# Ten chunks of the down projection's second column pass, beside the up projection

## The chip, the core and the metric

The kernel runs on one core of a Trainium2 chip. The metric is the device time of one launch in microseconds, as the median of several runs. The core's engines are TensorE (PE in the profile, with PEld for its weight loads), VectorE (DVE), ScalarE (ACT), GpSimd (POOL) and SyncE (SP). Each runs its own list of instructions in order and waits for others by semaphores; DMA transfers are issued here from the queues of SP and POOL.

## What is computed

One decoder layer for 256 tokens with 2048 features, in float32: a combined projection, two kinds of attention, an output projection, a LayerNorm, and a gated feed-forward network with a short causal convolution, followed by a second LayerNorm. The change lies in the feed-forward part:

```python
def conv_ffn(h, w_up, conv_w, conv_b, w_down):
    u = h @ w_up                                   # 256 x 2048 by 2048 x 11264
    g, val = u[..., :FFN_DIM], u[..., FFN_DIM:]    # FFN_DIM = 5632
    S = h.shape[1]
    gp = jnp.pad(g, ((0, 0), (CONV_W - 1, 0), (0, 0)))
    gc = conv_b + sum(conv_w[j] * gp[:, j:j + S] for j in range(CONV_W))
    return (jax.nn.silu(gc) * val) @ w_down        # 256 x 5632 by 5632 x 2048
...
h = layer_norm(DEEPNORM_ALPHA * h + mix, ln1_g[l], ln1_b[l])
f = conv_ffn(h, w_up[l], conv_w[l], conv_b[l], w_down[l])
h = layer_norm(DEEPNORM_ALPHA * h + f, ln2_g[l], ln2_b[l])
```

## The kernel before

**Precision.** Every float32 operand is split into a high part (`hi`, a rounded copy that ScalarE makes) and a low part (`lo`, the remainder, a subtraction on VectorE). A product is then three matmuls: high by high, high by low, low by high. `split_hi` and `split_lo` do this for the weights.

**The order of the work** is written out by hand. A list `stream` names the weight tiles one after another: value, query and key, output, up (88 tiles, gate and value of 44 feature blocks in turn) and down projection. A step works on one tile `i`, while the tile `i + 2` is split and `i + 5` or `i + 6` is loaded, so weights are ready two steps ahead.

**The up projection** takes 88 steps (`up_step`), each with 16 pairs of matmuls (512 and 256 columns) in `up_products`. ScalarE copies the result out of its PSUM bank (`up_copy`, tile `ub`), VectorE adds its two halves (`up_sum`), and the convolution and the gate follow (`gate_in`, `gate_taps`, `gate_out`, `act_out`). Two blocks of 128 features make a pair `p` of activations, one for every four steps, kept in a ring of three.

**The down projection** multiplies 22 pairs (chunks of 256 rows of `w_d`) by the weights, in two passes: first columns 0 to 1023 (n = 0), then 1024 to 2047 (n = 1). For one chunk and pass the product is a 2 x 2 by 2 x 2 block product. It is done either with eight block products (24 matmuls of 512 columns, `mm_d`), or, by Strassen's scheme in Winograd's form, with seven (21 matmuls), which needs four sums of weight blocks (tiles `tf`, split into `tslot`) and four sums of activations (tile `sf`, split into `sp`); `SEVEN` says which chunks do so. Seven of PSUM's banks collect the results: CB[0][0], CB[0][1], CB[1][0] and the four in MB, whose contents are shared by several outputs and added into `z` at the end of a pass by `shared_out`.

**Where the two meet.** The chunks 0 to 19 of the first pass run beside the up projection. Chunk `p` takes the four steps from 4 p + 8: `down_raw` loads its weights into one of two raw tiles (`raw` or a part of `ring`) two chunks ahead, the step before prepares the first sums, and after a step's up products TensorE runs 5, 5, 5 and 6 of the 21 side products (`down_products`, cut by `CUTS`). The three raw weight blocks that are used directly go to `rslot`, whose low parts are made by a DMA that accumulates (POOL, line 1166). `act_spill` writes the split activations (`dparts`) and, for five chunks, their split sums (`dsums`) to DRAM. After the up projection come chunks 20 and 21 of the first pass, and then the whole second pass: 22 chunks, of which five use seven products, with the activations read back by `act_back` (tiles `back`, `sback`). The last four chunks are ordered by output block, so that the LayerNorm of the first 128 tokens overlaps the end.

Two lines carry most of this:

```python
SEVEN = {"v": ((), range(1, 8, 3)), "d": (range(PT - 2), range(3, 16, 3))}
...
for j, p in enumerate((*range(PT - LATE, PT), PT - LATE - 1, *range(PT - LATE - 1))):
    stream.append(("d", p, 1, j))
```

## Time and profile before

| | us |
|---|---|
| median of 3 runs (1116.1 to 1117.8) | 1116.96 |
| the profiled execution | 1116.05 |
| its span in the profile | 1114.2 |
| TensorE busy | 1104.8 |
| VectorE busy | 853.8 |
| ScalarE busy | 681.5 |
| GpSimd busy | 57.4 |
| mean granted TensorE clock | 0.998 |

The profile comes from one execution. Its time is 1116.05 us, of which the span covers 1114.2. A row of a timeline gives the start, the duration, the engine and line, the operation and "out<-in" by the tiles' names, and how often it is repeated. A group row gives the total busy time, the mean duration in nanoseconds and the idle time ahead of it. The table of windows gives for each stretch the busy time of each engine with its count of instructions, the granted clock, the DMA engines' share and the rate. The rows themselves stand in the prediction.

### The profile page before, as it was taken

How to read it: one execution, taken by the hardware profiler on the slowest of the kernel's cores; microseconds unless marked ns; L12 is line 12 of the kernel's file. 1: busy time of each engine (PE TensorE's matmuls, PEld its weight loads, DVE VectorE, ACT ScalarE, POOL GpSimd, SP SyncE). 2: the span in 40 equal slices, each digit the busy share in tenths (PEclk: the TensorE clock that was granted, in tenths of full speed). 3: DMA queues.
4: the chain of work that ended last, by engine and by line, in shares of the span. 5: the costliest groups of instructions: out<-in, count | busy, mean ns of one | idle time of the engine just before them, and what ended most of it. 6: DMA issues, size and time to landing. Idle time of an engine off the chain costs nothing.

```text
span 1114.2 us, 15765 instructions
## 1 busy us (share of the span) xinstructions
PE 1104.8 (99%) x5929; PEld 952.9 (86%) x5929; DVE 853.8 (77%) x1400; ACT 681.5 (61%) x1077; POOL 57.4 (5%) x81
## 2 busy tenths in 40 slices
PE   9999999999999999999999999999999999999997
PEld 6888888888888898888888888888888888888886
DVE  6777778887755778888888887777777777677866
ACT  6656676655443486666666666666666666644552
POOL 0000010000000000000000000000000000001103
PEclk9999999999999999999999999999999999999999
DMA  9888866445455537877877877778777777688982
GB/s 326 286 286 308 245 195 209 151 158 183 159 182 189 189 119 260 300 247 246 275 257 257 270 246 250 250 241 261 248 249 243 247 249 245 199 321 289 330 324 77
DMA packets 59868, 266.46 MB, mean 239 GB/s; under 512 B 6080, under 2 KB 7568, under 8 KB 42000
## 3 DMA queue, kind: packets, MB, share of 16 engines
q1 hardware_dynamic: 51584, 229.81, 57.4%
q0 software_dynamic: 8064, 35.39, 14.1%
q8 instruction: 46, 0.75, 0.3%
q10 hardware_dynamic: 144, 0.26, 0.1%
q14 instruction: 30, 0.25, 0.1%
HBM read 227.93 MB, written 15.20 MB: 218 GB/s over the span
## 4 chain that ended last, share of the span: by engine, by line
PE 98%; DVE 1%; DMA 0%; ACT 0%; issue 0%; SPq 0%; DVEq 0%
PE bank L277 97%; PE bank L410 0%; DMA raw<-in_w_v 0%; PE bank L995 0%; PE bank L457 0%; ACT hf L998 0%; DVE h L1010 0%; DVE st L481 0%; DVE z L478 0%; DVE z L1357 0%; DVE z L1353 0%; DVEq L1505 0%; DVE mv L487 0%; ACT hi L208 0%; DVE h L1009 0%
## 5 line engine op out<-in xcount | busy, mean ns | idle before, releaser
L277 PE MATMUL bank<-h,hi 128*128 128x512 f32 x1376 | 480.9, 391 | 0.0
L277 PE MATMUL bank<-h,lo 128*128 128x256 f32 x1376 | 388.2, 282 | 0.0
L277 PEld LDWEIGHTS bank<-h,hi 128*128 128x128 f32 x1376 | 258.4, 188 | 54.1
L277 PEld LDWEIGHTS bank<-h,lo 128*128 128x128 f32 x1376 | 260.5, 189 | 3.7
L179 DVE TENSOR_TENSOR lo<-raw,hi 128x1024 fp32r<-128x1024 f32 x147 | 177.0, 1222 | 84.0 <-ACT hi L177 83.4
L196 DVE TENSOR_TENSOR lo<-raw,hi 128x1024 fp32r<-128x1024 f32 x171 | 207.0, 1221 | 25.0 <-ACT hi L188 24.8
L177 ACT ACTIVATE hi<-raw 128x1024 fp32r<-128x1024 f32 x155 | 161.7, 1056 | 75.8 <-PE bank L277 49.8
L277 PE MATMUL bank<-x,hi 128*128 128x512 f32 x512 | 182.9, 398 | 0.0
L188 ACT ACTIVATE hi<-raw 128x1024 fp32r<-128x1024 f32 x171 | 177.3, 1050 | 0.0
L277 PE MATMUL bank<-x,lo 128*128 128x256 f32 x512 | 144.4, 282 | 0.0
L1115 ACT ACTIVATE ub<-bank 128x512 f32<-128x512 f32 x86 | 51.4, 598 | 107.5 <-PE bank L277 104.5
L277 PEld LDWEIGHTS bank<-x,hi 128*128 128x128 f32 x512 | 96.3, 188 | 20.4 <-issue 1.0
L277 PEld LDWEIGHTS bank<-x,lo 128*128 128x128 f32 x512 | 97.0, 189 | 0.2
L1124 DVE TENSOR_TENSOR ub<-ub 128x256 f32<-128x256 f32 x86 | 36.5, 424 | 56.5 <-ACT ub L1115 56.5
L748 ACT ACTIVATE tslot<-tf 128x512 fp32r<-128x512 f32 x80 | 50.3, 629 | 44.1 <-DVE tf L1205 25.1
L751 DVE TENSOR_TENSOR tslot<-tf,tslot 128x512 fp32r<-128x512 f32 x80 | 55.3, 691 | 12.4 <-ACT tslot L748 10.3
L277 PE MATMUL bank<-hi,back 128*128 128x512 f32 (+1 forms) x216 | 59.0, 382 | 0.0
L277 PE MATMUL bank<-hi,x 128*128 128x512 f32 x208 | 55.9, 391 | 0.7 <-ACT hi L208 0.7
L277 PE MATMUL bank<-tslot,sp 128*128 128x512 f32 x180 | 47.8, 392 | 0.0
L277 PEld LDWEIGHTS bank<-hi,x 128*128 128x128 f32 x208 | 38.8, 188 | 9.6 <-ACT hi L208 1.7
L277 PEld LDWEIGHTS bank<-hi,back 128*128 128x128 f32 x216 | 40.2, 188 | 7.8
L277 PE MATMUL bank<-hi,mh 128*128 128x512 f32 x128 | 41.6, 396 | 0.0
(233 smaller groups left out, 1461.4 us busy)
## 6 DMA issues: line engine op xcount, KB each, us to landing
raw<-in_w_u SPq DMA_DIRECT2D x88, 1024.0 KB, 6.2
raw<-in_w_d SPq DMA_DIRECT2D x68, 512.0 KB, 7.3
raw<-in_w_qk SPq DMA_DIRECT2D x32, 1024.0 KB, 4.9
raw<-in_w_o SPq DMA_DIRECT2D x16, 1024.0 KB, 4.7
raw<-in_w_v SPq DMA_DIRECT2D x28, 512.0 KB, 7.3
ring<-in_w_d SPq DMA_DIRECT2D x20, 512.0 KB, 7.2
dparts<-rslot SPq DMA_DIRECT2D x20, 512.0 KB, 2.8
back<-dparts POOLq DMA_DIRECT2D x19, 512.0 KB, 7.3
```

What stands on the lines that cost most here:

```text
L177: ACT.activation(hi[:, s], t[:, x:y], AF.Copy)
L179: DVE.tensor_tensor(lo[:, s], t[:, x:y], hi[:, s].bitcast(F32), ALU.subtract)
L188: ACT.activation(hi, t[:, half * 1024:half * 1024 + 1024], AF.Copy)
L196: DVE.tensor_tensor(lo, t[:, half * 1024:half * 1024 + 1024], hi.bitcast(F32), ALU.subtract)
L277: PE.matmul(out, lhsT, rhs, start=start, stop=stop)
L748: ACT.activation(side["t"][:, 0, j], f, AF.Copy)
L751: DVE.tensor_tensor(side["t"][:, 1, j], f, side["t"][:, 0, j].bitcast(F32), ALU.subtract)
L1115: ACT.activation(t.rearrange("p j t -> p (j t)"), up_bank(i), AF.Copy)
L1124: DVE.tensor_tensor(u[:, 0], u[:, 0], u[:, 1], ALU.add)
```

## The change

Three things are changed together.

- Chunks 0 to 9 of the **second** pass now run beside the up projection's steps 8 to 45, with seven products each, in the place of the first pass; chunk 9 takes two steps instead of four. They are left out of the second pass, which keeps twelve chunks, two of them with seven products.
- At steps 46 to 49 the seven banks are added into `z` (`shared_out(1, ..., True)` and three `z_add`), while chunk 0 of the **first** pass begins. From step 50 to 87 there are then two chunks in four steps, each with 9 and 12 side products: a new one (10 to 19) with its activations at hand, and one of 1 to 9 whose activations and sums are read back from DRAM into a tile `more` (`act_reload`, POOL's queue). For these the low parts of `rslot` are made by VectorE (`r_hi`) and not by the accumulating DMA. The raw tile for the chunk after the next is asked for in a chunk's last step.
- The tiles `e0` and `e1` of the attention become places in one tile `e` (`e_place`), whose space `more` and `ends` use later; the offset `STAND_AT` of some stationary operands goes. The first sums for the last LayerNorm (`z_stats`) move two steps earlier in the shorter second pass.

```diff
-SEVEN = {"v": ((), range(1, 8, 3)), "d": (range(PT - 2), range(3, 16, 3))}
-
 LATE = 2

+EARLY = 10
+
+SEVEN = {"v": ((), range(1, 8, 3)), "d": (range(PT - LATE), (3, 6))}
...
-    for j, p in enumerate((*range(PT - LATE, PT), PT - LATE - 1, *range(PT - LATE - 1))):
+    for j, p in enumerate((*range(PT - LATE, PT), PT - LATE - 1, *range(EARLY, PT - LATE - 1))):
         stream.append(("d", p, 1, j))
...
         SP.dma_start(kept["parts"][p].bitcast(F32), side["x"].bitcast(F32))
-        if p in sevens:
+        if p < EARLY or p in sevens:
             SP.dma_start(kept["sums"][p].bitcast(F32), side["sp"].bitcast(F32))
...
-    def down_raw(p):
-        if p >= PT - 2:
+    jobs = []
+    for p in range(EARLY):
+        jobs.append((1, p, 4 * p + 8, 2 if p == EARLY - 1 else 4))
+    jobs.append((0, 0, 4 * EARLY + 6, 4))
+    for p in range(EARLY, PT - LATE):
+        jobs.append((0, p, 4 * p + 10, 2))
+        if p - EARLY + 1 < EARLY:
+            jobs.append((0, p - EARLY + 1, 4 * p + 12, 2))
+    FLUSH = EARLY
+
+    def fresh(j):
+        return jobs[j][1] >= EARLY or jobs[j][0] == 1
+
+    def steps(u):
+
+        for j, (_, _, first, length) in enumerate(jobs):
+            if first <= u < first + length:
+                k = 4 // length
+                return j, range((u - first) * k, (u - first + 1) * k)
+        return -1, range(u - 4, u - 3) if 4 <= u < 8 else range(0)
+
+    def down_raw(j):
+        if j >= len(jobs):
             return
...
+    def act_reload(j):
+
+        if j >= len(jobs) or fresh(j):
+            return
+        for t, src in zip(operands(j), (kept["parts"], kept["sums"])):
+            POOL.dma_start(t, src[jobs[j][1]])
...
-            np_ = pairs - (PAIRED_END if kind == "d" and n == 1 else 0)
+            np_ = pairs - (PAIRED_END + EARLY if kind == "d" and n == 1 else 0)
...
+    for m in (*MB, (0, 0), (0, 1), (1, 0)):
+        total[("d", "early", m) if m in MB else ("d", "early", *m)] = 3 * EARLY
...
-    CUTS = (0, 5, 10, 15, 21)
-
...
+    def cuts(j, u):
+
+        _, _, first, length = jobs[j]
+        if length == 2:
+            c = (0, 9, 21)
+        elif j == FLUSH:
+            c = (0, 0, 7, 14, 21)
+        else:
+            c = (0, 5, 10, 15, 21)
+        return c[u - first], c[u - first + 1]
...
+        if j == FLUSH and 0 in now:
+            shared_out(1, 0, True)
+        if j == FLUSH and 1 in now:
+            shared_out(1, 1, True)
+        if j == FLUSH and 2 in now:
+            for t, c in ((1, 0), (0, 0), (0, 1)):
+                z_add(1, t, c, CB[t][c])
...
+        if 3 in now:
+            down_raw(j + 2)
+        if 1 in new:
+            act_spill(jobs[j][1])
+        if 0 in now:
+            act_reload(j + 1)
...
+    def r_hi(j, x, y):
+
+        w, r = raw_of(j)[:, x:y], side["r"]
+        ACT.activation(r[:, 0, x:y], w, AF.Copy)
+        if not fresh(j):
+            DVE.tensor_tensor(r[:, 1, x:y], w, r[:, 0, x:y].bitcast(F32), ALU.subtract)
...
-                        at(i + 6 + 3 * t, z_stats, t, c, (512, 256)[t])
+                        at(i + 4 + 3 * t, z_stats, t, c, (512, 256)[t])
```

The other parts of `up_step` do what they did before, with "the chunk's step 0 to 3" (`0 in now` and so on, `now` being one or two of them) in place of "the step's place in its group of four", and with the sums of activations left out for a chunk that is read back (`new`, `fresh`).

**TensorE, in the second half of the up projection.** Before, a chunk's side products stand at the ends of four steps, after that step's matmuls with `h` (two rows of which are kept here):

```order
L277 MATMUL bank_74<-h_3405,hi 128x512
L277 MATMUL bank_74<-h_3405,lo 128x256
L277 MATMUL bank_76<-tslot,sp 128x512 x3
L277 MATMUL bank_78<-tslot,sp 128x512 x2
...
L277 MATMUL bank_78<-tslot,sp 128x512
L277 MATMUL bank_77<-tslot,sp 128x512 x3
L277 MATMUL bank_73<-tslot,rslot 128x512
...
L277 MATMUL bank_73<-tslot,rslot 128x512 x2
L277 MATMUL bank_75<-rslot 128x512 x3
```

In the changed kernel, at the ends of three steps, a new chunk's last twelve, then the first nine and the last twelve of a chunk that is read back:

```order
L279 MATMUL bank_73<-tslot,rslot 128x512 x3
L279 MATMUL bank_75<-rslot 128x512 x3
L279 MATMUL bank_71<-rslot 128x512 x3
L279 MATMUL bank_72<-rslot,sp 128x512 x3
...
L279 MATMUL bank_76<-tslot,more 128x512 x3
L279 MATMUL bank_78<-tslot,more 128x512 x3
L279 MATMUL bank_77<-tslot,more 128x512 x3
...
L279 MATMUL bank_73<-tslot,more 128x512 x3
L279 MATMUL bank_75<-rslot,more 128x512 x3
L279 MATMUL bank_71<-rslot,more 128x512 x3
```

The runs of side products are longer, two chunks share four steps, and every second chunk takes its activations from `more`.

**VectorE, in the step that follows a chunk's first step.** Before, in such a step of the second half (its third of four; `ub` is the sum of the step's halves, `lo` the low part of up weights, `tf` and `tslot` the sums of blocks for the next chunk):

```order
L1124 TENSOR_TENSOR ub<-ub 128x256
L557 TENSOR_TENSOR ring<-ub,gc 128x256
L196 TENSOR_TENSOR lo<-raw,hi 128x1024 x2
L1205 TENSOR_TENSOR tf<-raw 128x512
L751 TENSOR_TENSOR tslot<-tf,tslot 128x512 x2
```

In the changed kernel, in the second step of a chunk that is read back:

```order
L1184 TENSOR_TENSOR ub<-ub 128x256
L198 TENSOR_TENSOR lo<-raw,hi 128x1024
L561 SCALAR_TENSOR_TENSOR gc<-ub,vec,gc 128x255
L562 SCALAR_TENSOR_TENSOR gc<-ub,vec,gc 128x254
L198 TENSOR_TENSOR lo<-raw,hi 128x1024
L1364 TENSOR_TENSOR rslot<-raw,rslot 128x1024
L1309 TENSOR_TENSOR tf<-ring 128x512
L806 TENSOR_TENSOR tslot<-tf,tslot 128x512 x2
L1317 TENSOR_TENSOR tf<-ring,tf 128x512
L812 TENSOR_TENSOR sp<-sf,sp 128x256
L806 TENSOR_TENSOR tslot<-tf,tslot 128x512
```

The work of two former steps stands in one, and the low parts of `rslot` (line 1364) are new on this engine.

**SyncE's queue, in the second half.** Before, between two raw tiles of the down projection stand the loads of four weight tiles of the up projection:

```order
L126 DMA ring<-in_w_d 128x2x512
L127 DMA ring<-in_w_d 128x1024
L153 DMA raw<-in_w_u 128x2048 x2
L508 DMA dparts<-rslot 128x1024
L153 DMA raw<-in_w_u 128x2048 x2
L126 DMA raw<-in_w_d 128x2x512
L127 DMA raw<-in_w_d 128x1024
```

In the changed kernel stand two:

```order
L128 DMA ring<-in_w_d 128x2x512
L129 DMA ring<-in_w_d 128x1024
L155 DMA raw<-in_w_u 128x2048 x2
L128 DMA raw<-in_w_d 128x2x512
L129 DMA raw<-in_w_d 128x1024
L155 DMA raw<-in_w_u 128x2048
L519 DMA dparts<-rslot 128x1024
L155 DMA raw<-in_w_u 128x2048
```

The raw tiles come twice as often, and the activations are written out once in four steps as before.

More of the change, by code (lines that the diff above doesn't have):

```diff
@@ L368, in scores @@
         for j in range(n):
-            e = work.tile([P, 3 * P], F32, name=f"e{j}", bufs=3)
+            e = e_place(j)
             sb = score_banks(h)[j]
@@ L1257, in z_add, with shared_out @@
         DVE.tensor_tensor(z[:, t, s], z[:, t, s], src, ALU.add)
-    def shared_out(n, part):
+    def shared_out(n, part, early=False):
         if part == 0:
-            kept["u"] = work.tile([P, 512], F32, name="u", tag="sh", bufs=1)
+            kept["u"] = kept["gb"] if early else work.tile([P, 512], F32, name="u", tag="sh", bufs=1)
         u = kept["u"]
@@ L1274, in shared_out, with up_step @@
             z_add(n, 1, 1, u)
+    def up_step(i):
+        q, s = divmod(i - first_u, 4)
+        j, now = steps(i - first_u)
+        nxt = now if j + 1 < len(jobs) else ()
+        new = now if j >= 0 and fresh(j) else ()
+        if j < 0:
+            now = new = ()
+        f = (i - 1 - first_u) // 2
+        up_products(i)
+        u = None
+        if i == first_u + 3:
+            gate_in(0, bank[0][:, 0:S])
+            gate_taps(0, bank[0][:, 0:S])
+        if i > first_u + 2:
+            u = up_sum(i - 1)
+            if s % 2 == 0:
+                act_out(f, u)
+        if j == FLUSH and 0 in now:
[5 more added lines that the diff above has]
+                z_add(1, t, c, CB[t][c])
+        split_hi(i + 2, 0)
+        if s % 2 == 1 and u is not None:
+            gate_in(f, u)
+        if 0 in now:
+            if "r" not in side:
+                t = keep.tile([P, 4096], F32R, name="rslot", tag="big")
+                side["r"] = t[:, 0:3072].rearrange("p (a b c) -> p a b c", b=3, c=512)
+                side["x"] = t[:, 3072:].rearrange("p (a t) -> p a t", t=S)
+            w = raw_of(j)
+            if fresh(j):
+                ACT.activation(side["r"][:, 1], w[:, 0:3], AF.Copy, scale=-1.0)
+                POOL.dma_start(side["r"][:, 1], w[:, 0:3], accum_op=ALU.add)
+            DVE.tensor_tensor(side["f"][0], w[:, 1], side["f"][0], ALU.subtract)
+        if 0 in new:
+            s_hi(1)
+        split_lo(i + 2, 0)
+        if s % 2 == 1 and u is not None:
+            gate_taps(f, u)
+        if i == first_u + 3:
+            gate_out(0)
+            act_out(0, bank[0][:, S:2 * S])
+        if 0 in now:
+            t_hi(3, side["f"][0])
+        if 0 in new:
+            s_lo(1)
+        split_hi(i + 2, 1)
+        if s % 2 == 1 and u is not None:
+            gate_out(f)
+        if 0 in now:
+            t_lo(3, side["f"][0])
+        if s == 0 and 2 <= q < 10:
+            h_piece(q - 2, 0)
+        if 1 in new:
+            x, y = act_pair(jobs[j][1]), side["x"]
+            for h in (1, 0):
+                ACT.activation(y[:, 2 * h], x[:, h], AF.Copy)
+                DVE.tensor_tensor(y[:, 2 * h + 1], x[:, h], y[:, 2 * h].bitcast(F32), ALU.subtract)
+        if 1 in now:
+            r_hi(j, 0, 1)
+        split_lo(i + 2, 1)
+        if 1 in nxt:
+            if j < 0:
+                down_tiles()
+            w = raw_of(j + 1)
+            DVE.tensor_tensor(side["f"][0], w[:, 0], w[:, 3], ALU.subtract)
+            if fresh(j + 1):
+                down_act_sums(jobs[j + 1][1])
+        if 2 in now:
+            r_hi(j, 1, 3)
+        if 2 in nxt:
+            w = raw_of(j + 1)
+            t_hi(0, side["f"][0])
+            DVE.tensor_tensor(side["f"][1], w[:, 3], w[:, 2], ALU.add)
+            t_lo(0, side["f"][0])
+            t_hi(1, side["f"][1])
+            t_lo(1, side["f"][1])
+        if s == 2 and 2 <= q < 10:
+            h_piece(q - 2, 1)
+        if 3 in nxt:
+            w = raw_of(j + 1)
+            DVE.tensor_tensor(side["f"][0], w[:, 2], side["f"][0], ALU.subtract)
+            if fresh(j + 1):
+                s_hi(0)
+            t_hi(2, side["f"][0])
+            if fresh(j + 1):
+                s_lo(0)
+            t_lo(2, side["f"][0])
+        if i == first_d - 2:
+            split_act(first_d, 0)
+        if i == first_d - 1:
+            split_act(first_d, 1)
+            split_act(first_d + 1, 0)
+        if i == first_u + 2:
+            act_ring()
+            down_raw(0)
+        if q == 1 and s == 0:
+            down_raw(1)
+        if 3 in now:
+            down_raw(j + 2)
+        if 1 in new:
+            act_spill(jobs[j][1])
+        if 0 in now:
+            act_reload(j + 1)
+        if s == 2 and 1 <= q < 9:
+            load_piece(q - 1)
+        if 2 in now and j == (len(jobs) - 1) // 2 * 2:
+            turn.insert(0, side["raw"][1])
+            load(i + 5)
+        load(i + (5 if len(turn) == 3 else 6))
+        if i == first_d - 1:
+            load_gb(2, keep.tile([P, 2, D], F32, name="gb2", tag="ma"))
+        if now:
+            if 0 in now:
+                side["products"] = list(down_products(j))
+            x, y = cuts(j, i - first_u)
+            for key, dst, lhs, rhs in side["products"][x:y]:
+                mm_count(key, dst, lhs, rhs)
+        up_copy(i)
+        done(i)
```

178 lines of the change are left out of this document (48 added, 130 removed).

## The prediction

> **What bounds the kernel now.** I read the page first for the engine that is never idle, then the chain that ended last, then TensorE's own waits.
>
> ```profile
> PE 1104.8 (99%) x5929; PEld 952.9 (86%) x5929; DVE 853.8 (77%) x1400; ACT 681.5 (61%) x1077; POOL 57.4 (5%) x81
> ...
> PE 98%; DVE 1%; DMA 0%; ACT 0%; issue 0%; SPq 0%; DVEq 0%
> ```
> ```profile
> 405.98 698.84 PE bank L277 x3741
> 1104.82 0.02 issue
> ```
> ```profile
> PE bank L277 <- DVE idle L794: 1.2, 1, 1.2
> PE bank L277 <- ACT hi L208: 0.7, 1, 0.7
> PE bank L277 <- DVE h L1010: 0.7, 1, 0.7
> PE bank L1424 <- DVE cols L1423: 0.5, 1, 0.5
> PE bank L277 <- ACT side L1425: 0.4, 1, 0.4
> ```
>
> TensorE makes up 98% of the chain. From 406.0 us to 1104.8 us the chain is one row of 3741 matmuls, with nothing else between them, and all that TensorE waits for in the whole run is 3.5 us, at the start and at the tail. Both stages that the change touches, the up projection and the down projection's second pass, lie inside that one row. So the time there is the number of matmuls times their spacing, as long as no other engine gets in the way. A matmul's own duration (0.39 us) is no price, since matmuls overlap; the price is the distance between starts.
>
> ```profile
> 976.86 0.62 PE L277 MATMUL bank<-hi,ah 128*128 128x512 f32 x2
> ...
> 987.74 0.61 PE L277 MATMUL bank<-hi,ah 128*128 128x512 f32 x2
> ```
> ```profile
> 847.28 1.31 PE L277 MATMUL bank<-tslot,sp 128*128 128x512 f32 x5
> 848.43 0.39 PE L277 MATMUL bank<-h,hi 128*128 128x512 f32 x1
> ...
> 867.38 0.85 PE L277 MATMUL bank<-rslot 128*128 128x512 f32 x3
> ...
> 874.31 1.31 PE L277 MATMUL bank<-tslot,sp 128*128 128x512 f32 x5
> ```
> ```profile
> 843.78 0.86 POOL L1166 DMA_DIRECT2D rslot<-ring  x1 [26.17 <-ACT sp L754]
> 870.81 0.86 POOL L1166 DMA_DIRECT2D rslot<-raw  x1 [26.16 <-ACT sp L754]
> ```
>
> In the second pass 24 rows of two lie between 976.86 and 987.74: 48 matmuls in 10.88 us, 0.2267 us each. In the up projection five side products take 848.43 - 847.28 = 1.15 us, which is 5 x 0.2267 plus 0.02 us for entering the run. Six side products and one step's 32 up products take 874.31 - 867.38 = 6.93 us. One period of four steps (one chunk) is 870.81 - 843.78 = 27.03 us, with 5 + 5 + 5 + 6 side products: 3 x 1.15 + 1.38 = 4.83, which leaves 22.2, or 5.55 us for a step's up products.
>
> **What the change removes and adds on TensorE.** In the second column pass 5 chunks of 22 use seven products of three matmuls (21) and 17 use eight (24): 5 x 21 + 17 x 24 = 513. Afterwards ten chunks run early, all with 21, and of the twelve left two have 21 and ten have 24: 210 + 42 + 240 = 492. The 21 matmuls fewer are the whole gain: 21 x 0.2267 = **4.76 us**. The early ones are moved, not removed. Entering a run costs 0.02 us, and the number of runs hardly changes: 20 x 4 = 80 before; 9 x 4 + 2 + 3 + 19 x 2 = 79 after. If each side product cost 1.15 / 5 = 0.230 also in the longer runs, the 210 moved ones would cost 0.7 us more; that is the other end of this term, 4.06 us. I take 4.76, since the excess sits at the entry of a run. [...]
>
> **What must stay hidden.** The first half of the up projection keeps its rhythm (a chunk in four steps), only with other columns. Each early chunk writes its sums to DRAM too; the rows for that transfer are below and nothing near it waits. The critical place is the second half: 19 chunks of two steps each, 9.5 periods of four steps with two chunks. TensorE's time for such a period is 22.2 + 42 x 0.2267 + 4 x 0.02 = 31.8 us. VectorE is the nearest engine.
>
> ```profile
> core 0: us, PE busy (x) PEld busy (x) DVE busy (x) ACT busy (x) POOL busy (x), PEclk, DMA share, GB/s
> 470.00:497.00 27.00, 27.00 (x150) 23.61 (x150) 22.19 (x36) 18.15 (x28) 0.86 (x1) 1.00 0.77 253
> ...
> 848.00:875.00 27.00, 27.00 (x151) 23.61 (x149) 21.12 (x33) 18.15 (x28) 0.86 (x1) 1.00 0.77 244
> ```
> ```profile
> L196 DVE TENSOR_TENSOR lo<-raw,hi 128x1024 fp32r<-128x1024 f32 x153 | 185.2, 1221 | 22.8 <-ACT hi L188 22.7
> ...
> L751 DVE TENSOR_TENSOR tslot<-tf,tslot 128x512 fp32r<-128x512 f32 x74 | 51.1, 691 | 11.7 <-ACT tslot L748 9.8
> L748 ACT ACTIVATE tslot<-tf 128x512 fp32r<-128x512 f32 x74 | 46.5, 629 | 40.3 <-DVE tf L1205 22.2 <-DVE tf L1213 18.1
> ...
> L1201 ACT ACTIVATE rslot<-ring 128x1024 fp32r<-128x1024 f32 x10 | 10.5, 1049 | 0.0
> ...
> L1197 DVE TENSOR_TENSOR tf<-raw 128x512 f32<-128x512 f32 x9 | 6.2, 686 | 0.0
> ...
> L1191 ACT ACTIVATE rslot<-ring 128x512 fp32r<-128x512 f32 x10 | 6.2, 616 | 0.0
> ...
> L1257 DVE TENSOR_TENSOR z<-z,bank 128x512 f32<-128x512 f32 x6 | 3.8, 682 | 0.8 <-PE bank L277 0.8
> ```
> ```profile
> 853.08 1.22 DVE L196 TENSOR_TENSOR lo<-raw,hi 128x1024 fp32r<-128x1024 f32 x1
> 854.22 0.69 DVE L1197 TENSOR_TENSOR tf<-raw 128x512 f32<-128x512 f32 x1
> 854.82 0.42 DVE L762 TENSOR_TENSOR sf<-ring 128x256 f32<-128x256 f32 x1
> ```
> ```profile
> DVE ub L1124 <- ACT ub L1115: 50.4, 54, 3.1
> DVE lo L196 <- ACT hi L188: 21.2, 47, 0.5
> DVE rslot L1190 <- ACT rslot L1189: 15.6, 18, 1.1
> DVE tslot L751 <- ACT tslot L748: 8.9, 34, 0.4
> ```
>
> VectorE is busy 21.1 us of a period (in the first periods 22.2, with the pieces of the residual). The second chunk of a dense period is read back from DRAM already split, so it has no sums or splits of the activations; it adds four block sums (686 ns), four low parts (691 ns), and the low parts of three raw blocks in one operation of 512 and one of 1024 columns (nearest rows 691 and 1221 ns), which a DMA does for the other chunk: 2.74 + 2.76 + 1.91 = 7.4 us. Started back to back an operation costs about 0.09 us less than its duration (1.22 us at 853.08, the next at 854.22), so ten cost 6.6 us. That makes 27.7 to 28.5 us of 31.8. The waits in the last fence, from 500 to 980 us (17.8 periods), are 96 us, 5.4 a period, but 2.8 of these end with the copy of a step's own result, that is with TensorE: VectorE had run out of work. The other 2.6 are waits for ScalarE inside a step. So 27.7 + 2.6 = 30.3 us against 31.8: it fits, with 1.5 us to spare. ScalarE has 18.1 us now and gets four casts of 0.63 and the raw casts, 0.62 + 1.05: about 22.3. Momentary lateness is covered too: weights are split two steps before use, and a side product runs only after its step's 5.55 us of up products.
>
> At the turn between the passes, eleven adds from or to z (0.68 us each) empty seven banks: 7.5 us of VectorE in four steps that last 22.2 + 4.8 = 27.0 us on TensorE, with one chunk's work beside them: 21.1 + 7.5 = 28.6 us at most. The 1.6 us over is taken up by the two steps of lead. Cost 0 to 1.6 us; I take 0, as nothing near it has run out of lead.
>
> **Transfers.**
>
> ```profile
> raw<-in_w_d SPq DMA_DIRECT2D x20, 512.0 KB, 6.6
> ring<-in_w_d SPq DMA_DIRECT2D x18, 512.0 KB, 6.7
> ...
> dsums<-sp SPq DMA_DIRECT2D x4, 512.0 KB, 3.9
> ```
> ```profile
> DMA to landing us min/median/max: 5.2/6.8/8.6
> ```
> ```profile
> 859.37 0.46 SPq L126 DMA_DIRECT2D ring<-in_w_d  x1
> ```
> ```profile
> 880.95 0.69 DVE L1197 TENSOR_TENSOR tf<-ring 128x512 f32<-128x512 f32 x1
> ```
>
> A raw tile is asked for at 859.37 and first read at 880.95: 21.6 us for a landing of 5 to 9 us. In the dense half it is released late in a chunk's second step and first read late in the next step, which I put at one step (31.8 / 4 = 8.0 us) plus 1: 9 us. The bytes of a period grow from 27.0 x 244 = 6.6 MB by one raw load and one chunk read back, 2.1 MB, to 8.7 MB in 31.8 us, 273 GB/s; the DMA share goes from 0.77 to about 0.86. The landing should stay under 9 us, most of the time. SP's queue keeps its order (raw pair, then weights), POOL's gets two reads behind each accumulation, needed two steps later. A raw chunk that comes 1 us late costs VectorE spare time first.
>
> **Sum.** The profiled execution took 1116.05 us (1114.2 of span and 1.85 around it): 1116.05 - 4.76 = 1111.3. It lies 0.9 under the median of the three runs, 1116.96, so I forecast 1116.96 - 4.76 = **1112.2 us**.
>
> **Rivals.**
>
> *VectorE cannot overlap its operations in the dense half.* If about half of the 33 operations of a period now overlap by 0.09, whole durations make 21.1 + 1.4 + 7.4 = 29.9 us, and the 2.6 of waits 32.5 against 31.8: 0.7 x 9.5 = 6.6 us, which eats the gain: 1118.8 (1116 to 1121), no change. The overlap at 853.08 to 854.82 speaks against it; that more waits come with more operations speaks for it. [...]
>
> *VectorE's waits do not shrink (the slower side).* If all its idle time, 27.03 - 21.1 = 5.9 us a period, belonged to the hand-over between ScalarE and VectorE, the dense period would be 27.7 + 5.9 = 33.6 us, 1.8 over TensorE's: 9.5 x 1.8 = 17 us, so 1129. It decides once the waits pass 31.8 - 27.7 = 4.1 us. For it: each low part waits for its high part. Against it: half of the idle time is the wait for TensorE's result.
>
> *The raw tiles come late.* At a landing of 11 us each chunk would be 2 us late, VectorE's 1.5 us of spare time a period covers half, and about 1 us a chunk reaches TensorE: 19 us, 1131. It decides from about 10 us. Against it: no landing of these rows passes 8.6. For it: the share of 0.86.
>
> *Short stalls* at the turn and where the last dense chunk meets the second pass, 1 to 3 us: 1113.6 to 1115.
>
> **How the numbers follow.** Forecast 0.68 (1110.6 to 1113.6, with the 0.7 of the runs and the 0.9 by which single runs differ), short stalls 0.08, no overlap 0.09, waits 0.08, late tiles 0.07. About 0.2%, 2.2 us, is what a measurement of this kernel can tell from no change. Faster: 0.68 + 0.08 = 0.76; the same: 0.09; slower: 0.15. The range takes in the first two cases and the lower part of the third: 1110.6 to 1118.
>
> **What would show it.** TensorE's chain after 406 us still one row, with 3720 matmuls and 694 us. Dense periods of 31.8 us; VectorE busy near 28 in them, its wait for the copy of a step's result still there, though shorter. If dense periods are 32.5 or longer and VectorE shows no such wait, it has become the bound; if its first block sum of a chunk waits for a raw transfer, the tiles are late. A spacing other than 0.2267 in the long runs would mis-size the one term.

## The result, and the profile after

The changed kernel is **slower**: 1124.47 us as the median of 6 runs (1123.69 to 1125.68) against 1116.93 for the kernel before (6 runs, 1116.10 to 1117.80). The ratio is 1.0069, with an interval of 1.0058 to 1.0079. The forecast was 1112.2 with a range up to 1118.0, so both the sign and the range were wrong. The profiled execution took 1124.31 us, with a span of 1122.5 and a mean granted clock of 0.995.

The page of the changed kernel, its busy times and its chain:

```profile
PE 1106.5 (99%) x5908; PEld 949.5 (85%) x5908; DVE 889.0 (79%) x1470; ACT 692.2 (62%) x1109; POOL 61.8 (6%) x88
...
PE 84%; DVE 8%; ACT 4%; issue 2%; DMA 2%; SPq 0%; ACTq 0%; DVEq 0%
```

TensorE runs 5908 matmuls, 21 fewer than 5929, as counted. But it makes up 84% of the chain and no longer 98%: VectorE, ScalarE and transfers now stand in it. Busy time alone does not show the loss: TensorE is still busy 99% of the span, with more microseconds for fewer matmuls. Here is the list of what TensorE waited for in the changed kernel (total us, times, longest):

```profile
PE bank L279 <- ACT ub L1175: 3.6, 2, 2.9
PE bank L279 <- ACT end L179: 1.6, 1, 1.6
...
PE bank L279 <- DVE end L181: 0.8, 1, 0.8
```

These three rows are new. They make 6.0 us. That is less than what was lost, since the kernel grew by 8.3 us of span (1122.5 against 1114.2) although 4.76 us of matmuls went: some 13 us have to be found. A waits list names only gaps. To find the rest I use a mark that every step of the up projection from the third on leaves: ScalarE's copy of the step's result (`ub<-bank`, 86 of them, line 1175). Three of them in the timeline of the changed kernel, for the steps 46, 50 and 87:

```profile
700.66 0.60 ACT L1175 ACTIVATE ub<-bank 128x512 f32<-128x512 f32 x1 [1.21 <-PE bank L279]
...
733.24 0.60 ACT L1175 ACTIVATE ub<-bank 128x512 f32<-128x512 f32 x1 [1.38 <-PE bank L279]
...
1030.37 0.60 ACT L1175 ACTIVATE ub<-bank 128x512 f32<-128x512 f32 x1 [1.76 <-PE bank L279]
```

They cut the time after step 46 into three stretches: the **turn** between the passes (733.24 - 700.66 = 32.58 us), the **dense half** (1030.37 - 733.24 = 297.13) and the **tail**, up to the end of the last long run of matmuls in the chain (1113.03 - 1030.37 = 82.66). What each would be with TensorE never held up follows from the prediction's prices: the turn 4 x 5.55 + 21 x 0.2267 + 3 x 0.02 = 27.0; the dense half 37 steps with 387 side products, 205.4 + 87.7 + 0.7 = 293.8 (the kernels in which nothing holds it show 293.63, which I use); the tail 342 matmuls at 0.2267 = 77.5, and the 0.6 by which the tail of the kernel before (129.13 us for 567 matmuls) was longer than its own count: 78.1.

| us | turn | dense half | tail |
|---|---|---|---|
| without a hold-up | 27.0 | 293.6 | 78.1 |
| changed kernel | 32.58 | 297.13 | 82.66 |
| lost | 5.5 | 3.5 | 4.5 |

Lost are 13.5 us. Ahead of step 46 the changed kernel gained 0.6: its copy of step 46 comes 1.9 us later than before (700.66 against 698.78), with eleven more side products of chunk 9 (2.5 us) done by then. That 0.6 is not the change's doing: it is there at the first of the 86 copies already (408.19 against 408.81), and over all kernels here that copy lies anywhere from 408.2 to 409.8. So 13.5 - 0.6 - 4.76 = 8.1 us, and the span shows 8.3.

**The dense half.** One period of four steps in the chain of the changed kernel (start, duration, engine, what):

```profile
823.84 21.74 PE bank L279 x117
845.65 0.60 ACT ub L1175
846.25 0.96 ACT hi L190
847.23 1.23 DVE lo L198
849.89 0.96 ACT rslot L1362
850.87 1.23 DVE rslot L1364
852.10 0.61 DVE tf L1309
852.79 0.65 ACT tslot L803
853.50 0.57 issue
854.07 0.70 DVE tf L1317
855.39 0.59 ACT ub L1175
856.02 21.74 PE bank L279 x117
```

For most of a period the chain is TensorE, then in one step of four it runs through ScalarE and VectorE and comes back to TensorE by `ub`, the copy. From 823.84 to 856.02 are 32.18 us, against the 31.8 predicted; nine such periods make the 3.5 us. ScalarE's own rows in that step show what delays the copy (in brackets the idle time before, and what ended it):

```profile
854.85 0.64 ACT L803 ACTIVATE tslot<-tf 128x512 fp32r<-128x512 f32 x1 [1.12 <-DVE tf L1317]
855.39 0.58 ACT L1175 ACTIVATE ub<-bank 128x512 f32<-128x512 f32 x1
```

ScalarE sat idle for 1.12 us, with the copy in its list right behind the cast. The up products that the copy needs had ended long before, at 852.88 + 0.28 = 853.16, as TensorE's rows show, with the last of the side products:

```profile
852.88 0.28 PE L279 MATMUL bank<-h,lo 128*128 128x256 f32 x1
...
853.69 2.20 PE L279 MATMUL bank<-rslot,more 128*128 128x512 f32 x9
856.02 0.50 PE L279 MATMUL bank<-h,hi 128*128 128x512 f32 x1
```

The cast (`tslot<-tf`) waits for a block sum of VectorE (line 1317), and the copy waits behind it. The next step's first matmul, at 856.02, writes the same PSUM bank that the copy empties: from the up projection's ninth step on, all its steps use bank 3. So TensorE has no two steps of lead towards the copy. It has the length of that step's side products, 12 x 0.2267 = 2.7 us, and then it stands. The gap in TensorE's rows is too short for the list of waits, which has no row for it. The chain and the step marks do show it.

The kernel before used the same one bank, with a shorter lead (five side products, 1.15 us), and lost nothing. There ScalarE came to the copy in time: ahead of each of the 37 copies from step 50 to step 86 it sat idle for 0.51 us or more. The tightest step of a period looks like this:

```profile
867.59 0.60 ACT L1115 ACTIVATE ub<-bank 128x512 f32<-128x512 f32 x1 [0.52 <-PE bank L277]
```

ScalarE waited for TensorE and had 0.52 us to spare. In the changed kernel 18 of the 37 copies have no such idle time ahead of them, and in the step shown the copy starts 2.2 us after the up products have ended.

### The profile page after: what moved, and what is told of

It reads as the page before. It is cut to its first block, busy times and chain, and to the rows that moved or that the text cites. A ratio compares the mean times of both kernels' runs of the same rounds, so it can differ in the third digit from the quotient of the medians.

```text
span 1122.5 us, 15881 instructions
## 1 busy us (share of the span) xinstructions
PE 1106.5 (99%) x5908; PEld 949.5 (85%) x5908; DVE 889.0 (79%) x1470; ACT 692.2 (62%) x1109; POOL 61.8 (6%) x88
## 4 chain that ended last, share of the span: by engine, by line
PE 84%; DVE 8%; ACT 4%; issue 2%; DMA 2%; SPq 0%; ACTq 0%; DVEq 0%
PE bank L279 83%; DVE lo L198 1%; DVE rslot L1364 1%; ACT ub L1175 1%; DMA raw<-in_w_d 1%; ACT rslot L1362 1%; ACT hi L190 1%; DVE z L1211 1%; ACT tslot L803 1%; DVE tf L1309 1%; DVE tf L1317 1%; PE bank L421 0%; DVE lo L181 0%; DMA raw<-in_w_v 0%; DVE gc L562 0%
## 5 line engine op out<-in xcount | busy, mean ns | idle before, releaser
L198 DVE TENSOR_TENSOR lo<-raw,hi 128x1024 fp32r<-128x1024 f32 x171 | 207.6, 1220 | 19.8 <-ACT hi L190 19.6
L181 DVE TENSOR_TENSOR lo<-raw,hi 128x1024 fp32r<-128x1024 f32 x133 | 160.3, 1221 | 70.9 <-ACT hi L179 70.1
L179 ACT ACTIVATE hi<-raw 128x1024 fp32r<-128x1024 f32 x141 | 147.6, 1057 | 67.1 <-PE bank L279 46.5
L190 ACT ACTIVATE hi<-raw 128x1024 fp32r<-128x1024 f32 x171 | 178.2, 1050 | 0.0
L803 ACT ACTIVATE tslot<-tf 128x512 fp32r<-128x512 f32 x120 | 74.4, 627 | 76.9 <-DVE tf L1317 35.4
L806 DVE TENSOR_TENSOR tslot<-tf,tslot 128x512 fp32r<-128x512 f32 x120 | 82.0, 690 | 23.2 <-ACT tslot L803 21.3
L565 ACT ACTIVATE gc<-gc 128x256 f32<-128x256 f32 x44 | 18.4, 418 | 36.8 <-DVE gc L562 36.8
L279 PE MATMUL bank<-lo,mh 128*128 128x512 f32 x128 | 40.8, 390 | 0.0
```

The lines of the kernel that those rows point to most:

```text
L179: ACT.activation(hi[:, s], t[:, x:y], AF.Copy)
L181: DVE.tensor_tensor(lo[:, s], t[:, x:y], hi[:, s].bitcast(F32), ALU.subtract)
L190: ACT.activation(hi, t[:, half * 1024:half * 1024 + 1024], AF.Copy)
L198: DVE.tensor_tensor(lo, t[:, half * 1024:half * 1024 + 1024], hi.bitcast(F32), ALU.subtract)
L279: PE.matmul(out, lhsT, rhs, start=start, stop=stop)
L565: ACT.activation(gates[f], gates[f], AF.Silu)
```

## The experiments

Each kernel is the changed one with the edit that is shown. All times in one table, in the stretches defined above; the excess is that of the median over the kernel before, run beside it on the same chip.

| kernel | turn | dense half | tail | median | excess | ratio (95%) |
|---|---|---|---|---|---|---|
| changed | 32.58 | 297.13 | 82.66 | 1124.47 | +7.5 | 1.0069 (1.0058 to 1.0079) |
| e1_sevens_2_5 | 33.90 | 297.12 | 84.63 | 1127.02 | +10.6 | 1.0090 (1.0072 to 1.0108) |
| e2_copy_first | 31.17 | 293.63 | 80.46 | 1120.61 | +4.2 | 1.0035 (1.0021 to 1.0049) |
| e3_no_turn_adds | 28.03 | 297.13 | 80.59 | 1119.16 | +2.7 | 1.0024 (1.0014 to 1.0035) |
| e4_both | 31.19 | 293.62 | 83.89 | 1121.09 | +4.6 | 1.0045 (1.0029 to 1.0061) |
| e5_turn | 27.81 | 293.63 | 82.37 | 1116.59 | +0.3 | 1.0001 (0.9991 to 1.0011) |
| e6_places_early | 32.75 | 293.63 | 79.90 | 1119.34 | +3.0 | 1.0029 (1.0020 to 1.0038) |
| e7_all | 27.81 | 293.62 | 79.92 | 1114.07 | -2.2 | 0.9978 (0.9967 to 0.9988) |
| e8_one_seven | 32.75 | 293.63 | 78.72 | 1117.69 | +1.4 | 1.0010 (1.0001 to 1.0019) |
| f1_turn_one_seven | 27.81 | 293.63 | 78.70 | 1112.87 | -3.3 | 0.9966 (0.9953 to 0.9978) |
| f2_all_casts_behind | 28.82 | 293.06 | 82.80 | 1118.05 | +1.9 | 1.0018 (1.0009 to 1.0028) |
| f3_spread_only | 27.64 | 297.19 | 80.47 | 1119.48 | +3.3 | 1.0026 (1.0016 to 1.0036) |

The stretches come from one profiled execution each, the medians from 4 to 10 runs.

### The dense half: is it the copy's place, or VectorE's load?

Two theories. Either the copy stands behind a cast that waits for VectorE, and it is enough to put it ahead; or VectorE with its 27.7 us of work a period is too slow, and the order does not matter. In this kernel the last sums and casts of a chunk's fourth part stand behind the copy, with all their operations:

```diff
-        if 3 in nxt:
-            w = raw_of(j + 1)
-            DVE.tensor_tensor(side["f"][0], w[:, 2], side["f"][0], ALU.subtract)
...
         up_copy(i)
+        if 3 in nxt:
+            w = raw_of(j + 1)
+            DVE.tensor_tensor(side["f"][0], w[:, 2], side["f"][0], ALU.subtract)
...
```

> Edit: in each step of the up projection ScalarE copies the finished bank out before it casts the last sum of blocks for the next chunk, instead of after. Theory 'one bank': the up projection has a single PSUM bank, so the next step's first matmul waits for that copy, and the copy waits in ScalarE's queue behind a cast that waits for VectorE; the dense period falls from 32.17 to 31.8 us (3 us in all), and the turn between the passes loses a part of its 5.5 us: 3 to 5 us less than the changed kernel, 1119.5 to 1121.5. Rival 'VectorE is full': the order on ScalarE does not matter, the dense period stays at 32.2 and the time within 1 us of 1124.5.

The chain of this kernel has one row from the turn through the whole dense half and 13 us into the tail:

```profile
720.21 320.06 PE bank L279 x1701
```

The dense half takes 293.63 us, and from the copy of step 50 to that of step 86 286.08, which is 9 x 31.79: the predicted period to 0.01 us. VectorE does the same work: its operations come in the same order in both traces, and only ScalarE's come in another. The table of windows, first of the changed kernel, then of this one (length, busy time of PE, PEld, DVE, ACT and POOL with counts, granted clock, DMA share, GB/s):

```profile
760.00:1016.00 256.00, 255.14 (x1357) 218.95 (x1357) 220.25 (x343) 172.55 (x263) 15.75 (x24) 1.00 0.81 271
```
```profile
760.00:1010.00 250.00, 250.00 (x1340) 216.86 (x1340) 216.81 (x338) 170.84 (x259) 15.72 (x24) 1.00 0.82 276
```

VectorE is busy 86.0% of the time in the one and 86.7% in the other, or 27.7 us of a period of 32.2 and 27.6 of 31.8. With as much work on it TensorE does not wait. So VectorE is not the bound of the dense half, and the place of one copy in ScalarE's list is worth its 3.5 us. The time of 1120.61 lies in the range that was expected, but not all of the gain is the edit's. The wait of 2.9 us at the turn is still there, because the cast ahead of the copy is there one of a chunk's third part, which this edit does not move. The turn is 1.4 us shorter, and the tail 2.2, mainly because the granted clock stayed at 1.00 behind the waits, where in the changed kernel it was 0.54 from 720 to 722 us and 0.50 from 1094 to 1096 (last section). The turn and the tail remain.

### The turn: the additions, the order, or both?

At the end of the turn's third step, step 48, ScalarE's rows in the changed kernel are these:

```profile
717.59 0.63 ACT L803 ACTIVATE tslot<-tf 128x512 fp32r<-128x512 f32 x1 [6.28 <-DVE tf L1309]
718.13 0.58 ACT L1175 ACTIVATE ub<-bank 128x512 f32<-128x512 f32 x1
```

VectorE's, over the same time:

```profile
711.62 1.87 DVE L1211 TENSOR_TENSOR z<-z,bank 128x512 f32<-128x512 f32 x3
...
715.68 1.22 DVE L1364 TENSOR_TENSOR rslot<-raw,rslot 128x1024 fp32r<-128x1024 f32 x1
716.82 0.68 DVE L1309 TENSOR_TENSOR tf<-ring 128x512 f32<-128x512 f32 x1
```

And TensorE's:

```profile
715.27 0.61 PE L279 MATMUL bank<-rslot,more 128*128 128x512 f32 x2
718.76 0.80 PE L279 MATMUL bank<-h,hi 128*128 128x512 f32 x1 [2.88 <-ACT ub L1175]
```

It is the same bank and the same copy. The block sum (line 1309) for which the cast waits comes late, because VectorE first does three of the eleven additions into `z`, two low parts of up weights (left out here), and a low part of `rslot` which before was made by a DMA. ScalarE stands idle for 6.28 us, TensorE for 2.88. The question is which of these counts. The first kernel leaves all the additions out:

```diff
-        if j == FLUSH and 0 in now:
-            shared_out(1, 0, True)
-        if j == FLUSH and 1 in now:
-            shared_out(1, 1, True)
-        if j == FLUSH and 2 in now:
-            for t, c in ((1, 0), (0, 0), (0, 1)):
-                z_add(1, t, c, CB[t][c])
```

> Edit: the eleven additions into z (and the copy) at the turn between the passes, steps 46 to 49, are left out, so the early chunks' products are missing from the output. Theory: these VectorE additions cost the 5.5 us by which the four steps exceed their matmuls; without them 5 to 6 us less, about 1119, and the granted clock in this stretch is back at 1.00. Rival: the turn is slow because chunk 0's data come back from DRAM late or because of its low parts on VectorE: less than 2 us gained.

The turn falls from 32.58 to 28.03: the additions cost 4.55 of the 5.5 us, the wait of 2.9 and the slower clock behind it. The other 1.0 us stays: step 46 has no side products, and TensorE waits 0.7 us for its copy, with or without the additions. The dense half stays at 297.13, as it must if that loss has another cause.

A kernel that has to add them anyway can spread them over the four steps, behind the low part of the next weights, let the first products of chunk 0 start earlier (3, 6, 6 and 6 instead of 0, 7, 7 and 7) and make that chunk's low parts by DMA. This kernel does so, and puts both blocks of sums and casts behind the copy besides:

```diff
+    def turn_adds(k):
+        u = kept.get("u")
+        if k == 0:
+            shared_out(1, 0, True)
+        elif k == 1:
+            z_add(1, 0, 1, u)
+            DVE.tensor_tensor(u, MB[7], u, ALU.add)
...
-            c = (0, 0, 7, 14, 21)
+            c = (0, 3, 9, 15, 21)
...
-            if fresh(j):
+            if fresh(j) or j == FLUSH:
...
+        if j == FLUSH and now:
+            turn_adds(now[0])
...
         up_copy(i)
+        if 2 in nxt:
...
+        if 3 in nxt:
...
```

> Edit on the kernel with the copy first: all casts of the next chunk's block sums now stand behind the copy on ScalarE, the eleven additions of the turn are spread over its four steps (4, 2, 3, 2) behind each step's first weights, the 21 side products of the turn over four runs of 3, 6, 6, 6, so that no step lacks the products that cover the copy, and chunk 0's low parts are made by the accumulating DMA. Theory 'turn': the four steps come from 31.2 us (copy first alone) to 27 to 28 us, the dense period stays at 31.8: about 4 us less than copy first alone, 1116 to 1117.5. Rival 'VectorE is full at the turn': its work of some 28 us does not fit whatever the order, and the four steps stay above 29.5 us.

The turn takes 27.81 us, 0.8 over what the matmuls alone need, and the dense half 293.63. The time is that of the kernel before; the gain of 4.76 us is now given back in the tail (82.37). To see which half of this edit does it, one kernel has the order alone and one the spreading alone:

```diff
         up_copy(i)
+        if 2 in nxt:
...
+        if 3 in nxt:
...
```

> Edit on the changed kernel: only the order on ScalarE, the casts of all of the next chunk's block sums behind the copy; the additions of the turn, its products and chunk 0's low parts stay as in the changed kernel. Theory 'order': at the turn too it is the copy behind a waiting cast that stops TensorE; then the four steps come to 28 us, as in the spread kernel. Theory 'load': the additions keep VectorE itself late, and a tile of sums that it has not yet read keeps the copy back; then the four steps stay above 29.5 us and the spreading was needed.

```diff
...
+        if j == FLUSH and now:
+            turn_adds(now[0])
...
-            c = (0, 0, 7, 14, 21)
+            c = (0, 3, 9, 15, 21)
...
-            if fresh(j):
+            if fresh(j) or j == FLUSH:
...
```

> Edit on the changed kernel: only the turn (additions and products spread, chunk 0's low parts by DMA); the order on ScalarE stays as in the changed kernel. By both theories the dense period stays at 32.17 us. Theory 'order': the four steps stay above 29.5 us, as the casts still stand ahead of the copy. Theory 'load': they come to 28 us.

Spreading alone brings the turn to 27.64, so the order is not needed there. The order alone takes away the wait of 2.9 us at the end of step 48 and brings the turn to 28.82, between the two values that were expected. But 1.6 us more are then lost just ahead of it, and TensorE waits 2.3 us for the copy of step 46, because ScalarE has this row shortly before that copy:

```profile
702.35 0.63 ACT L803 ACTIVATE tslot<-tf 128x512 fp32r<-128x512 f32 x1 [3.31 <-DVE tf L1269]
```

This cast belongs to chunk 0 itself (its last block sum, line 1269, behind four of the additions on VectorE), and the edit leaves it ahead of the copy. So at the turn less work for VectorE ahead of the block sums is enough, and in the dense half the order is needed (the spread kernel without it stays at 297.19). Whether the order would be enough at the turn too, with this cast also behind the copy, was not tried, and the three parts of the spreading (additions, products, low parts by DMA) were not tried one by one. In both places the rows show one mechanism, the copy queued behind a cast that waits for VectorE.

### The tail: where chunks with seven products stand

The chain of the changed kernel in the tail runs over VectorE and ScalarE from 1044 to 1078 us, and then over a transfer:

```profile
1044.36 0.68 DVE z L1211
...
1074.26 1.48 ACT slot L666
1075.77 1.77 DVE slot L667
1078.97 11.89 DMA raw<-in_w_d
1090.97 1.06 ACT end L179
1092.06 1.24 DVE end L181
1093.33 19.70 PE bank L279 x101
```

It begins with the additions that end the first pass (`shared_out`), goes on through the block sums of the two chunks with seven products, and VectorE does not catch up. Lines 666 and 667 split the three weight blocks that a chunk with seven products uses directly, here those of the chunk at place 6 of the second pass; only then is its raw tile free. SP's queue asks for the next tiles right behind, for the last one in two transfers:

```profile
1078.54 0.38 SPq L128 DMA_DIRECT2D raw<-in_w_d  x1
1078.97 0.63 SPq L129 DMA_DIRECT2D raw<-in_w_d  x1
```

The last one lands 11.89 us later, longer than any raw tile of the dense half took (9.4 at most), with the DMA engines' share at 0.93 to 1.12 from 1082 to 1088 us. TensorE stands still twice, for the high and for the low part:

```profile
1092.08 0.50 PE L279 MATMUL bank<-end,slot 128*128 128x512 f32 x1 [1.58 <-ACT end L179]
1093.33 2.04 PE L279 MATMUL bank<-end,slot 128*128 128x512 f32 x5 [0.76 <-DVE end L181]
```

These two waits are 2.3 of the 4.5 us. Some 1.6 more come from a slower clock behind them: from 1093.9 to 1097.3 the matmuls start 0.43 us apart instead of 0.2267, with a granted clock of 0.50 from 1094 to 1096 us.

In the kernel before, the last chunk with seven products stands at place 15 of 22, six places from the end and 14 behind the first pass's additions, which are listed at the places 0 and 1. Here it stands at place 6 of twelve, five from the end and five behind them. The first trial moves both one place forward:

```diff
-SEVEN = {"v": ((), range(1, 8, 3)), "d": (range(PT - LATE), (3, 6))}
+SEVEN = {"v": ((), range(1, 8, 3)), "d": (range(PT - LATE), (2, 5))}
```

> Edit: the two chunks of the second pass that use seven products stand at places 2 and 5 instead of 3 and 6. The changed kernel's TensorE stalls 2.9 us before the last four chunks (its last raw tile lands at 1091, 12 us after it was asked for) and then runs at a slower clock for some 3 us; from the last up-projection copy to the end of the matmuls it takes 4.5 us more than the count of matmuls gives. Theory 'place': a chunk with seven products keeps its raw tile a step longer, and at place 6 this delays the request for the last tiles; with place 5 they are asked for one chunk (5 us) earlier: the stall and the slow clock go, 4.5 us less than the changed kernel, about 1120. Rival 'transfers': the queue is simply full in the shorter pass, and the last tile lands about as late: less than 1 us gained.

The time is 1127.02, not the 1120 of theory 'place'. The waits at the end are gone, but a longer one comes in. From this kernel's list of TensorE's waits:

```profile
PE bank L279 <- DVE u L1226: 4.2, 1, 4.2
```

Line 1226 is the addition that empties the last shared bank of the first pass. `shared_out` for it is listed at the places 0 and 1, but VectorE comes to it late, and a chunk with seven products at place 2 is to write those banks again. The tail is 84.63, longer than in the changed kernel. (The turn is longer too, though the edit does not touch it: there the granted clock is 0.50 to 0.57 from 720 to 726 us, behind the same wait of 2.9.) With the copy moved as well the two edits do not add up, because the new wait stays:

```diff
+SEVEN = {"v": ((), range(1, 8, 3)), "d": (range(PT - LATE), (2, 5))}
...
         up_copy(i)
+        if 3 in nxt:
...
```

> Edit: both the places 2 and 5 and the copy first, nothing left out. If the losses are independent, the gains of the two runs before add up: 7.5 to 9.5 us less than the changed kernel, 1115 to 1117. If one bound hides behind the other, less than the sum.

The tail is 83.89 with the wait of 4.2 us, and the time lies within the interval of the copy moved alone. So the next kernel has, beside these two edits, `shared_out` two places earlier, beside the last chunks of the first pass, which don't use those banks:

```diff
-        at(first_d + LATE + part, shared_out, 0, part)
+        at(first_d + part, shared_out, 0, part)
```

> Edit on the kernel with the copy first: the two chunks with seven products stand at places 2 and 5, and the additions of the first pass's shared banks are started two steps earlier, with the first chunk after the up projection. In the run with places 2 and 5 alone TensorE did not wait for the last tiles, but 4.2 us for just these additions before the chunk at place 2. Theory 'place': with the additions earlier neither wait is left, and from the last copy to the last matmul it takes 78 to 79 us (80.5 with copy first alone, 83.9 with both edits): 2 to 3 us less than copy first alone, about 1118. Rival: VectorE cannot do the additions and the sums of blocks in time, and a wait of over 2 us stays before the chunk at place 2.

The last tile is now asked for 43.9 us after the copy of step 87, and TensorE does not wait for it. But a wait of 1.5 us for another addition into `z` is left, so the tail is 79.90 and not the 78 to 79 that were expected. The last trial gives the second of the two chunks up, which puts three matmuls (0.68 us) back:

```diff
+SEVEN = {"v": ((), range(1, 8, 3)), "d": (range(PT - LATE), (3,))}
```

(together with the copy ahead of the fourth part's casts)

> Edit on the kernel with the copy first: only the chunk at place 3 of the second pass uses seven products, the one at place 6 eight: three matmuls (0.7 us) more. Theory 'place': without the chunk at place 6 no raw tile is held longer and the last tiles are asked for in time, so TensorE does not wait before the last four chunks: 80.5 + 0.7 - 2.4, about 79 us from the last copy to the last matmul. Rival 'transfers': the last tile lands late here too, and the wait of 1 to 2 us stays.

There is no wait at the end any more. SP's queue in this kernel asks for the last tile at 1071.38, 43.7 us after its copy of step 87; in the changed kernel that request comes 48.2 us after it (1078.54):

```profile
1071.38 0.38 SPq L128 DMA_DIRECT2D raw<-in_w_d  x1
```

and TensorE's chain, from the turn to the end of the matmuls, is one row:

```profile
719.45 386.99 PE bank L279 x2011
```

The tail is 78.72. Its 345 matmuls at 0.2267 and the 0.6 above make 78.8, so nothing is lost in it.

### Together

> Edit: both runs before together; nothing is left out of the computation. If the three losses (copy, turn, tail) are the whole difference from the count of matmuls, the time is the one that the count gives, 1111.5 to 1113.5, faster than the kernel before. If something else costs time (clock, transfers), it stays above 1114.

This one has the turn of `e5_turn` and the tail of `e6_places_early`: 1114.07, faster than before, but above the 1111.5 to 1113.5 that were expected, as the wait of 1.5 us in the tail is still there. The last has the turn of `e5_turn` and one chunk with seven products:

```diff
+SEVEN = {"v": ((), range(1, 8, 3)), "d": (range(PT - LATE), (3,))}
```

> Edit: the copy first and the turn spread as before, and one chunk with seven products, at place 3, in the second pass; nothing left out of the computation. By the parts: the turn kernel's steps up to the last copy (its profile: 1023.0), then the 78.7 us that the kernel with one seven took from there to its last matmul, against 79.9 with the places 2 and 5: 1113 us or a little less, 3 to 4 us under the kernel before. If the wait before the last four chunks comes back with the earlier turn, 1115 to 1117.

It takes **1112.87 us** (5 runs, 1112.51 to 1113.25) against 1116.14 beside it: a ratio of 0.9966 (0.9953 to 0.9978), faster than both kernels. Its page and its chain:

```profile
PE 1101.6 (99%) x5911; PEld 948.3 (85%) x5911; DVE 875.1 (79%) x1461; ACT 694.2 (62%) x1107; POOL 62.0 (6%) x88
...
PE 95%; DVE 2%; DMA 1%; issue 1%; ACT 0%; DVEq 0%; POOL 0%; POOLq 0%
```
```profile
708.37 393.49 PE bank L279 x2054
```

18 matmuls fewer than before are worth 4.08 us; the medians show 3.27, and the 0.8 that the turn still loses is about the rest.

## Why the prediction was wrong, by its steps

**The count and the price of the matmuls were right.** TensorE has 21 matmuls fewer, and where nothing holds it up a dense period takes 31.79 us, against 31.8 forecast (`e2_copy_first`). The gain is there: the best kernel, whose count is lower by 18, got 3.3 of its 4.08 us.

**VectorE's load in the dense half was right too.** Predicted were 27.7 us a period, measured 27.7 and 27.6. Its waits for ScalarE were put at 2.6 us a period. In `f1_turn_one_seven` they are 4.2 (32.8 us from 760 to 1010), nearly all of the 4.5 us that it is idle (31.8 less 27.3, from 214.81 us busy in 250). Yet there TensorE does not wait. So my test, that busy time plus waits must stay under TensorE's period (27.7 + 2.6 = 30.3 against 31.8), was no test: the waits stretch to fill the period, and the rival built on them (VectorE's waits do not shrink, 1129) had a point of decision, 4.1 us, that was passed without effect.

**The step that failed is "Momentary lateness is covered too: weights are split two steps before use".** That is true of the weights in these stages. It leaves out the one result that comes back in the other direction: a step's bank has to be emptied by ScalarE before the next step's first matmul. Towards that copy TensorE is ahead by the step's own side products, 2.7 us for twelve, 1.6 for seven and none for a step without them, as at the first step of the turn. The copy itself was never more than 0.1 us late in the dense half of the kernel before; in the changed one it waits up to 2.2 us behind a cast. I looked at how far ahead each input is made, and not at how far behind each output may be taken away. The dense half lost 3.5 us by it, and `e2_copy_first` shows that this was the whole of its loss.

**"The 1.6 us over is taken up by the two steps of lead. Cost 0 to 1.6 us; I take 0" failed for the same reason, and its size by more.** The balance of 28.6 against 27.0 us was over four steps; the additions stood in the first three of them, ahead of the block sum that holds up the cast that holds up the copy. VectorE's work as such would have fitted: it is 27.4 us in the turn of the changed kernel, and in `f1_turn_one_seven` 26.7 us of it stand in a turn of 27.81. The turn lost 5.5 us: waits of 2.9 and 0.7, some 1.4 by a slower clock behind the long one (below), and the rest at the edges of the waits. The rival "short stalls" had the two places, the turn and the second pass's beginning, at 1 to 3 us together.

**The second pass had no term at all.** I counted its matmuls and let it keep its rhythm. Shortening it from 22 places to twelve brought its last chunk with seven products close behind the first pass's additions and one place nearer to the end, so that VectorE released the last raw tiles late. The tail lost 4.5 us by that and by the clock behind it. This was not a term of the wrong size: it was put at nothing, without a reason.

**Right, though it did not matter: the transfers.** In the dense half the share of the DMA engines is 0.81 to 0.82 with 271 to 276 GB/s, against 0.86 and 273 forecast, and the raw tiles land in time (line 129 of the changed kernel, from 735 to 1020 us; the 11.9 us of the last tile belong to the tail):

```profile
DMA to landing us min/median/max: 5.2/7.4/8.9
```

Nor did I name the sign that would have told the causes apart. "If dense periods are 32.5 or longer and VectorE shows no such wait, it has become the bound" comes close to what the trace shows (32.18 us, and VectorE's wait for the copy down from 22.4 us in 200 us of the kernel before to 3.0 in 256), and it would have blamed the wrong engine.

Of the 0.8 us that the turn still loses in the best kernel, its trace shows the places. Step 46 has three side products (0.68 us) to cover its copy, and the next step begins 0.25 us late; and the first side product of step 47 waits for the addition that empties the last shared bank, which costs about 0.5 (the copies of steps 46, 47 and 48 start at 701.72, 708.22 and 715.67 us: 6.50 and 7.45 apart, against 6.25 and 6.93 by the matmuls). No run tried to win this back. It also stays open whether the seven-product chunk's raw tile alone made the last transfers late: in `e8_one_seven` that chunk's additions on VectorE went along with it.

## What to carry to other kernels

For every engine that is never idle, list not only what it waits for as input, but also which of its results must be taken away before it can go on, by whom, and what stands ahead of that in the taker's list; the lead is the shortest of these. In the list of an engine that works in order, as ScalarE did here (idle for 1.12 us, with a copy that had all it needed behind a cast that waited), put the operation that frees the bound engine's bank ahead of operations that wait for a third engine. And where a loop gets shorter, recompute how far from its end the last loads are asked for: what was covered by ten more rounds is here two waits of 2.3 us in all.

## What the runs showed of the hardware

Some stalls of TensorE cost more than their length here. The table of windows of the changed kernel, around the stall at 715.9 to 718.8 (the clock is the third column from the right):

```profile
718.00:720.00 2.00, 1.24 (x4) 1.05 (x5) 1.44 (x4) 2.00 (x4) 0.00 (x0) 0.61 0.96 403
720.00:722.00 2.00, 2.00 (x8) 1.73 (x7) 1.97 (x4) 1.17 (x3) 0.00 (x0) 0.54 0.95 315
722.00:724.00 2.00, 2.00 (x14) 1.75 (x13) 1.90 (x3) 0.99 (x3) 0.00 (x0) 1.00 0.68 236
```

And of `e2_copy_first`, right behind a stall of the same length that ends at 720.2:

```profile
720.00:722.00 2.00, 1.79 (x10) 1.59 (x11) 1.59 (x3) 2.00 (x4) 0.00 (x0) 1.00 0.84 342
```

In the changed kernel the granted clock is about half for some 3 us behind the stall, and only 8 matmuls stand in the 2 us from 720 to 722 where 14 stand in the next 2. That costs about 1.4 us, the difference between the turns of 32.58 and 31.17. Of the six kernels with a wait of 2.9 us at the turn, four show the drop (0.50 to 0.54 at the lowest, in steps of 2 us) and two (`e2_copy_first`, `e4_both`) do not (1.00 throughout), so stalls of this length went either way; the length of the drop differs too, nearly 6 us in `e1_sevens_2_5` (0.50 to 0.57 from 720 to 726 us), whose turn is 33.90. In the tail two stalls shortly behind one another did it too: 1.6 and 0.8 us in the changed kernel (clock 0.50 and 0.67 from 1094 to 1098), while 1.1 and 0.8 us in `e2_copy_first` left the clock at 1.00. The same 1.1 and 0.8 in `f2_all_casts_behind` dropped it (0.50 from 1090 to 1092 us), so there too the length alone does not decide. What does, no run shows.

ScalarE kept to the order of its list. In the changed kernel it sat idle for 1.12 us ahead of the cast at 854.85, and the copy behind that cast did not start before 855.39, although the up products that it needs had ended at 853.16. In `e2_copy_first`, whose list has the copy ahead of that cast, the period is 31.79 us and not 32.18.
